# Loads of two blocks moved to the ScalarE queue, and the first store moved up behind its Silu, in an RMSNorm + SiLU kernel

One core of one Trainium2 chip. The metric is the device time of one execution in microseconds (us), the median of several; lower is better.

## The reference

```python
# x: (8, 1024, 2048) float32, gamma: (2048,) float32, eps = 1e-5
rms = np.sqrt(np.mean(x ** 2, axis=-1, keepdims=True) + eps)
out = gamma * x / rms
return out * (1 / (1 + np.exp(-out)))
```

67.11 MB are read and 67.11 MB written; every element is used once.

## The kernel before

The 8192 rows are cut into 16 blocks of 4 MB (128 partitions x 4 rows x 2048). Six buffers hold blocks; a block is loaded, worked on in place and stored. The ring of buffers ties the two ends together: block b + 6 may be loaded only when block b has been stored.

```python
def load(b):
    xt = pool.tile([P, J * d], f32, name="xt")          # 6 buffers
    nc.sync.dma_start(out=xt, in_=xb[b])                # SyncE's queue
    blocks[b] = xt

def sums(b, after_first=()):                            # sums of squares
    ...                                                 # 1 or 2 rows on VectorE, 2 or 3 on ScalarE (Square)
        if j == 0:
            for s in after_first:
                store(s)                                # behind the block's first Square
    ...                                                 # rstd = (ss / d + eps) ** -0.5 on GpSimd

def finish(b, halves=False):
    ...                                                 # VectorE: x * rstd * gamma; ScalarE: Silu, 2 rows at a time

def store(b):
    nc.scalar.dma_start(out=ob[b], in_=blocks[b])       # ScalarE's queue
    if b + LEAD < nblk:                                 # LEAD = 6
        load(b + LEAD)

# start: five loads, gamma on ScalarE's queue, then load 5
for b in range(BUFS - 1):
    load(b)
...
sums(0); finish(0); sums(1)
for b in range(1, last - 1):
    sums(b + 1, after_first=[b - 1])
    finish(b)
...                                                     # the last block is stored in two halves
```

## Time and profile before

| | |
|---|---|
| time, first three runs | 317.98 us median (317.71 to 318.61) |
| span of the profiled run | 316.6 us |
| bytes moved | 134.24 MB, mean 424 GB/s |
| busy: VectorE, ScalarE, GpSimd | 67%, 60%, 20% |
| DMA packets' time, both queues | 98.7% of 16 engines' span |

The line of DMA shows for each fortieth of the span how busy the 16 DMA engines were, in tenths; below it is what they moved. It reads 9 nearly everywhere here, so the DMA engines are what binds, although compute engines wait too. The prediction shows these lines. In the views SPq and ACTq are the sequencers of SyncE and ScalarE, which issue the DMAs; "Square" and "Silu" are ScalarE's two operations (L68 and L86).

### The profile page before, as it was taken

What the parts mean: (1) busy time and instruction counts of PE and PEld (TensorE: products, weight loads), DVE (VectorE), ACT (ScalarE), POOL (GpSimd) and SP (SyncE); (2) the same over time, 40 slices, a digit from 0 to 9 for tenths busy, and PEclk for the clock granted to TensorE, in tenths of its full rate; (3) what the DMA queues carried; (4) which work ended last, traced back from release to release, by engine and by line L of the source; (5) the groups of instructions that cost most, each with busy time, mean ns of one, the idle gap of its engine ahead of it and who ended that gap; (6) DMA issues with size and microseconds to landing.
All of it is one profiled execution on the core that took longest, in us unless ns stands there. A gap on an engine that the chain in (4) does not pass through costs nothing.

```text
span 316.6 us, 446 instructions
## 1 busy us (share of the span) xinstructions
PE 2.1 (1%) x8; PEld 0.5 (0%) x8; DVE 212.5 (67%) x122; ACT 190.2 (60%) x107; POOL 64.6 (20%) x37
## 2 busy tenths in 40 slices
PE   0200000000000000000000000000000000000000
PEld 0000000000000000000000000000000000000000
DVE  0688599996772947929485393975929369985600
ACT  1338978688774285473778436567368754782800
POOL 0010160514040601506004060330602106001000
DMA  8999999999999999999999999999999999999995
GB/s 332 414 447 431 431 397 443 418 447 414 447 414 455 411 448 414 447 439 422 435 426 439 431 435 426 451 414 447 426 435 435 426 435 426 435 431 439 426 429 242
DMA packets 4762, 134.24 MB, mean 424 GB/s; under 512 B 532, under 2 KB 532, under 8 KB 536
## 3 DMA queue, kind: packets, MB, share of 16 engines
q1 hardware_dynamic: 2304, 67.11, 49.5%
q10 hardware_dynamic: 2456, 67.12, 49.2%
q14 instruction: 2, 0.02, 0.0%
HBM read 67.12 MB, written 67.11 MB: 424 GB/s over the span
## 4 chain that ended last, share of the span: by engine, by line
DMA 59%; DVE 15%; issue 4%; ACT 3%; DVEq 1%; POOL 0%; POOLq 0%; ACTq 0%; SPq 0%
DMA xt<-in_x_dram 35%; DMA out_dram<-xt 24%; DVE xt L82 13%; ACT xt L86 2%; DVE junk_v L64 1%; ACT junk_a L68 1%; DVEq L158 1%; POOLq L158 0%; POOL rstd L77 0%; ACTq L91 0%; DVE ss L64 0%; POOL var L74 0%; ACTq L68 0%; SPq L52 0%; DVEq L82 0%
## 5 line engine op out<-in xcount | busy, mean ns | idle before, releaser
L86 ACT ACTIVATE xt<-xt 128x4096 f32<-128x4096 f32 x32 | 115.7, 3617 | 71.4 <-DVE xt L82 71.4
L82 DVE SCALAR_TENSOR_TENSOR xt<-xt,rstd,g 128x2048 f32<-128x2048 f32 x64 | 146.1, 2346 | 8.7 <-POOL rstd L77 8.7
L64 DVE CUSTOM_DVE_ANT_0 junk_v<-xt 128x2048 f32<-128x2048 f32 x28 | 64.4, 2299 | 66.4 <-DMA xt<-in_x_dram 66.0
L68 ACT ACTIVATE junk_a<-xt 128x2048 f32<-128x2048 f32 x36 | 67.7, 1880 | 39.0 <-DMA xt<-in_x_dram 37.9
L74 POOL TENSOR_SCALAR var<-ss 128x4 f32<-128x4 f32 x16 | 22.4, 1401 | 222.1 <-DVE ss L64 117.5
L77 POOL TENSOR_TENSOR rstd<-var,half 128x4 f32<-128x4 f32 x16 | 41.9, 2621 | 1.3
L112 DVE COPY g<-junk_v 128x2048 f32<-128x2048 f32 x1 | 2.3, 2292 | 9.3 <-PE junk_v L110 9.3
L68 ACT ACTIVATION_READ_ACCUMULATOR junk_a<-xt 128x1 f32 x36 | 6.7, 186 | 0.0
L64 DVE DVE_READ_ACCUMULATOR2_ANT ss<- 128x1 f32 x28 | 3.9, 141 | 0.0
L110 PE MATMUL junk_v<-xt,ones 1*128 1x512 f32 x8 | 2.1, 1133 | 8.1 <-DMA xt<-in_gamma_dram 8.1
L105 ACT ACT_TABLE_LOAD x1 | 1.3, 1283 | 0.7 <-PEq L144 0.7
L86 ACT ACT_TABLE_LOAD x1 | 1.3, 1283 | 0.0
L103 DVE MEMSET ones<- 128x128 f32 x1 | 0.2, 165 | 0.8 <-PEq L144 0.8
L110 PEld LDWEIGHTS junk_v<-xt,ones 1*128 1x128 f32 x8 | 0.5, 305 | 8.1 <-issue 8.1
L105 ACT ACTIVATE junk_a<-ones 128x1 f32<-128x1 f32 x1 | 0.2, 174 | 0.0
L104 POOL MEMSET half<- 128x4 f32 x1 | 0.1, 101 | 0.3 <-POOLq L144 0.3
L144 POOL MEMSET const-float32-0.0<- 128x1 f32 x1 | 0.1, 98 | 0.2 <-issue 0.2
L144 POOL MEMSET const-bfloat16-1.0<- 128x1 bf16 x1 | 0.1, 101 | 0.0
L144 POOL MEMSET const-uint8-127<- 128x1 uint8 x1 | 0.1, 101 | 0.0
L144 POOL MEMSET const-float32-1.0<- 128x1 f32 x1 | 0.1, 99 | 0.0
## 6 DMA issues: line engine op xcount, KB each, us to landing
xt<-in_x_dram SPq DMA_DIRECT2D x16, 4096.0 KB, 36.9
out_dram<-xt ACTq DMA_DIRECT2D x15, 4096.0 KB, 40.1
out_dram<-xt ACTq DMA_DIRECT2D x2, 2048.0 KB, 14.0
xt<-in_gamma_dram ACTq DMA_DIRECT2D x1, 8.0 KB
```

What stands on the lines that cost most here:

```text
L64: nc.vector.tensor_tensor_reduce(out=junk_v, in0=row(b, j), in1=row(b, j), scale=1.0, scalar=0.0, op0=ALU.mult, op1=ALU.add, accum_out=ss[ ...
L68: nc.scalar.activation(out=junk_a, in_=row(b, j), func=ACT.Square, accum_out=ss[:, j:j + 1])
L74: nc.gpsimd.tensor_scalar(out=var, in0=ss, scalar1=1.0 / d, scalar2=float(eps), op0=ALU.mult, op1=ALU.add)
L77: nc.gpsimd.tensor_tensor(out=rstd, in0=var, in1=half, op=ALU.pow)
L82: nc.vector.scalar_tensor_tensor(out=row(b, j), in0=row(b, j), scalar=rstds[b][:, j:j + 1], in1=g, op0=ALU.mult, op1=ALU.mult)
L86: nc.scalar.activation(out=blocks[b][:, cols], in_=blocks[b][:, cols], func=ACT.Silu)
L103: nc.vector.memset(ones, 1.0)
L105: nc.scalar.activation(out=junk_a[:, 0:1], in_=ones[:, 0:1], func=ACT.Square)
L110: nc.tensor.matmul(junk_v[:, c * w:(c + 1) * w], ones[k:k + 1, :], grow[k:k + 1, 0:w], start=True, stop=True)
L112: nc.vector.tensor_copy(out=g, in_=junk_v)
L144: nc = _bacc.Bacc("TRN2", target_bir_lowering=False, num_devices=1)
L158: with _tile.TileContext(nc) as tc:
```

## The change

The intent: keep both DMA queues at work all the time. Before, ScalarE's queue carried nothing but gamma until the first store at 38 us. Now it carries blocks 1 and 3, and the first store comes right behind them as soon as its Silu is done.

```diff
-    def load(b):
+    def load(b, queue=None):
         xt = pool.tile([P, J * d], f32, name="xt")
-        nc.sync.dma_start(out=xt, in_=xb[b])
+        (queue or nc.sync).dma_start(out=xt, in_=xb[b])
...
-        for b in range(BUFS - 1):
-            load(b)
+        load(0)
...                                    # gamma's load on ScalarE's queue
+        for b in range(1, BUFS - 1):
+            load(b, nc.scalar if b in (1, 3) else nc.sync)
...
         sums(0)
         finish(0)
+        store(0)
         sums(1)
         for b in range(1, last - 1):
-            sums(b + 1, after_first=[b - 1])
+            sums(b + 1, after_first=[b - 1] if b > 1 else [])
```

## The prediction

> **What bounds the kernel now.** I read the page from the top: busy shares, slices of DMA, share of the two queues, and the chain of waits.
>
> ```profile
> PE 2.1 (1%) x8; PEld 0.5 (0%) x8; DVE 212.5 (67%) x122; ACT 190.2 (60%) x107; POOL 64.6 (20%) x37
> ...
> DMA  8999999999999999999999999999999999999995
> GB/s 332 414 447 431 431 397 443 418 447 414 447 414 455 411 448 414 447 439 422 435 426 439 431 435 426 451 414 447 426 435 435 426 435 426 435 431 439 426 429 242
> ...
> q1 hardware_dynamic: 2304, 67.11, 49.5%
> q10 hardware_dynamic: 2456, 67.12, 49.2%
> ...
> DMA 59%; DVE 15%; issue 4%; ACT 3%; DVEq 1%; POOL 0%; POOLq 0%; ACTq 0%; SPq 0%
> ```
>
> No compute engine is near full (VectorE 67%). The DMA digit is 9 in all slices but the first and the last, and the queues' packets take 49.5 + 49.2 = 98.7% of sixteen engines' span. The queue q1 is SyncE's (loads, 67.11 MB), q10 ScalarE's (gamma and stores, 67.12 MB). So the bound is moved bytes: 134.24 MB. The waits of the two sides confirm it: compute waits for loads, and SyncE, which issues the loads, waits for stores to free the buffers.
>
> ```profile
> DVE junk_v L64 <- DMA xt<-in_x_dram: 66.0, 12, 8.0
> ACT junk_a L68 <- DMA xt<-in_x_dram: 37.9, 11, 10.9
> ...
> SPq L52 <- DMA out_dram<-xt: 225.0, 10, 52.9
> ```
>
> Next I cut the span into stretches, to see where the DMA engines lose time (columns: stretch, its us, busy us and instructions of PE, PEld, DVE, ACT, POOL, then clock, DMA share, GB/s).
>
> ```profile
> 0.00:2.00 2.00, 0.00 (x0) 0.00 (x0) 0.17 (x1) 1.28 (x1) 0.29 (x5) 1.00 0.66 180
> 2.00:6.00 4.00, 0.00 (x0) 0.00 (x0) 0.00 (x0) 0.17 (x1) 0.00 (x0) 1.00 0.75 311
> ...
> 179.00:256.00 77.00, 0.00 (x0) 0.00 (x0) 52.40 (x30) 46.83 (x26) 19.02 (x8) 1.00 1.00 432
> ...
> 312.00:317.00 5.00, 0.00 (x0) 0.00 (x0) 0.00 (x0) 0.00 (x0) 0.00 (x0) 1.00 0.24 102
> ...
> 14.00:38.00 24.00, 0.00 (x0) 0.00 (x0) 19.99 (x14) 17.36 (x13) 1.21 (x2) 1.00 1.01 436
> 38.00:46.00 8.00, 0.00 (x0) 0.00 (x0) 6.44 (x3) 5.95 (x7) 4.76 (x4) 1.00 0.99 389
> 46.00:102.00 56.00, 0.00 (x0) 0.00 (x0) 42.42 (x25) 42.10 (x23) 14.06 (x7) 1.00 1.00 432
> ```
>
> The steady rate is about 433 GB/s, and it is the same with one queue working (436 in 14 to 38 us, loads alone) as with two (432). At 433 GB/s the bytes need 134.24 / 0.433 = 310.0 us. The span is 316.6, so 6.6 us are lost, and the stretches say where. **Start**: 0 to 6 us moved 2 x 180 + 4 x 311 = 1604 KB, worth 3.7 us, so 2.3 lost. **End**: 312 to 316.6 moved 510 KB, worth 1.2 us, so 3.4 lost. **A dip**: 38 to 46 us at 389 GB/s loses 8 x (433 - 389) / 433 = 0.8 us. Sum 6.5. The dip stands exactly where the first store is issued, onto a ScalarE queue that had carried only gamma:
>
> ```profile
> 33.90 0.18 ACT L68 ACTIVATION_READ_ACCUMULATOR junk_a<-xt 128x1 f32 x1
> ...
> 38.23 1.88 ACT L68 ACTIVATE junk_a<-xt 128x2048 f32<-128x2048 f32 x1
> ...
> 38.28 0.36 ACTq L91 DMA_DIRECT2D out_dram<-xt  x1
> ```
>
> That is the one loss in mid-run, and it bears on what the change is for.
>
> **What the Trainium skill says.** "DMA: Bandwidth & Descriptors", section "Issuing engines are not separate DMA queues": DMAs of all issuing engines end on the same 16 DMA engines and interleave; several issuers save only issue time. The trace agrees: 436 GB/s with one queue, 432 with two. The same page, "Queues, rings and completion order": each DMA engine takes turns between the queue rows it has work for, packet by packet. The trace agrees in that the steady stage gives a load of 4 MB a median of 36.9 us from issue to landing while the first load, alone, took 12.3. The same page, "Bandwidth", gives a fabric ceiling of 435 GB/s; the measured 433 leaves almost nothing between. No page that I found tells what the first transfer on an idle queue costs; the dip is only the trace's.
>
> **The change part by part.**
>
> 1. Blocks 1 and 3 go to ScalarE's queue, behind gamma; SyncE keeps 0, 2, 4 and 5. This adds two issues on ScalarE at about 0.34 us each (the stores' issue there is 338 ns), in the first 3 us when ScalarE waits for data until 13.09 anyway: nothing on the path. The bytes and their rate stay. But the order of arrival changes. A block alone takes 4.194 MB / 0.433 = 9.7 us; two queues taking turns bring two blocks in 19.4. Block 0, which landed at 13.1 alone, had perhaps 1 to 2 us alone ahead of block 1's start, so I expect it at 21 to 22 us, and block 1 some 1 us later; blocks 2 and 3 at 41 to 42. So the first sums start 8 us later.
>
> 2. The first store. Before, block 0's last Silu started at 28.58 and took 3.62, done at 32.2, 19.1 us after landing; its store waited until 38.28 behind four Squares of blocks 1 and 2, the first of which waited for ScalarE's turn at 32.10. Now it stands right behind the Silu: 21.4 + 19.1 = about 40.5 us. So it comes 2 us later, not earlier, in spite of being moved up. It costs nothing in DMA: loads fill the engines until about 60 us (six blocks of 9.7, plus the start). Block 3's tail on the ScalarE queue runs to about 42, and the store's packets, perhaps 2 us after issue (the estimate is from the first load, issued at 0.72 and moving within 2 us), would be there at about 42.4. So the queue is handed over nearly without a gap; I can't tell which side of zero.
>
> 3. The following stores. In the new order ScalarE does three Squares of block 1 (3 x 2.05 us), then two of block 2, Silu of block 1 and a Square of block 3 before store 1: rstd of block 1 at about 48.4, four VectorE passes to 57.5, second Silu done at about 61.2, store 1 issued at about 61.4 (52.38 before). Store 0 moves from 42.4 to 42.4 + 19.4 = 61.8, so store 1's packets may come 1 to 2 us after the ScalarE queue ran dry. Load 5 alone then keeps the engines busy; no bytes are lost except by a second dip, if waking a queue is what costs. By the same counting store 2 is issued at about 75 against a need at 82, store 3 at 89 against 102: compute has caught up.
>
> 4. From about 100 us on both kernels run the same loop. Store 0 lands at about 62 in both, so load 6 goes out at the same time, and the order of instructions on all engines is the same from the second store on.
>
> 5. The tail: the last two half stores were issued at 296.93 and 301.45, while the earlier stores had work until about 303, so the engines stayed full to 312. I expect the same slack of some 7 us.
>
> Sum: bytes 0; issue 0; later first compute 0, hidden under loads; dip between -0.8 (gone) and +0.8 (a second one); start -0.3 to +0.5 (two queues ramp together, or the second disturbs the first). My centre is half the dip won: 317.98 - 0.4 = **317.6 us**.
>
> **The rivals.**
>
> *A: the dip is the price of waking the ScalarE queue, and it vanishes into the start.* For it: the packets' rate falls exactly after the issue at 38.28, no later store makes such a stretch, and rates are lowest at the start too, where the other queue wakes. Then -0.8 us: 317.2.
>
> *B: the dip is the price of the first write, or of a mixture of reads and writes beginning, or it comes with the wake wherever that is.* Against it speaks only that I see no reason in the trace. Then it moves to 42 us or to 3 us, and the time is the same: 318.0.
>
> *C: the delayed compute of block 0 hits the path: the ScalarE queue runs dry, SyncE has no free buffer, both queues idle.* For it: 8 us of delay in the first landing, and store 1 nine us later. Against it: two blocks of loads (19 us) are still queued when store 0 starts, one remains when it ends. If I am wrong by some 10 us there, it would cost a few us: 320 to 323.
>
> *D: two queues really move more than one.* It would need more than the 432 of the mixed stage; the loads alone show 436. Worth at most 1% of 40 us, 0.4 us.
>
> **Range and chances.** The three times of before span 317.71 to 318.61, so noise alone is about half a microsecond. Between A with some of D (316.8) and B with a second dip (318.8) lies nearly everything; C has perhaps one chance in twenty. Faster by over 2% needs 6.4 us, and all that is lost besides bytes is 6.6, most of it start and end that the change leaves: 1%. Slower by 2% needs C in a bad form: 2%. Within 2%: 97%.
>
> **What would show it right or wrong.** Step 1: the first Square at 21 to 22 us instead of 13.09. Step 2: the first store's issue at 40 to 41. Step 3: the second at 60 to 62. Step 4: SyncE's waits for stores as large as before, and the DMA digit 9 throughout. The dip: GB/s in 38 to 46 us; 430 or more says A, about 390 says B; a new dip near 62 to 68 says that a queue that ran dry pays again. Step 5: the last store issued at about 301. The prediction is wrong if a digit under 9 shows up between 20 and 300 us (C), or if the mean rate in mid-run differs from 432.

## The result, and the profile after

After: 318.52 us median (318.36 to 319.36, 6 runs); before, over the six runs to that point: 318.38 us (317.71 to 319.63). The ratio is 1.0006, 95% interval 0.9985 to 1.0028: the same. Here and below a ratio is the mean time of one kernel's fast runs over that of the other's of the same rounds, so it is not quite the ratio of the medians.

The page of the changed kernel, to be held against the same lines of before:

```profile
DMA  8999999999999999999999999999999999999996
...
q10 hardware_dynamic: 2744, 75.51, 55.3%
q1 hardware_dynamic: 2016, 58.72, 43.6%
```

The two loads did move: 8.4 MB went from q1 (SyncE) to q10 (ScalarE). The sum of the shares is 98.9% against 98.7% before. There was no idle share to win.

The order of events in the changed kernel, from the timeline (start, duration, engine, line, operation):

```profile
20.25 1.88 ACT L68 ACTIVATE junk_a<-xt 128x2048 f32<-128x2048 f32 x1 [18.07 <-DMA xt<-in_x_dram]
...
35.74 3.62 ACT L86 ACTIVATE xt<-xt 128x4096 f32<-128x4096 f32 x1 [0.91 <-DVE xt L82]
...
39.38 0.36 ACTq L91 DMA_DIRECT2D out_dram<-xt  x1
...
60.09 0.35 ACTq L91 DMA_DIRECT2D out_dram<-xt  x1
```

Block 0 shares the engines with block 1 and lands at 20.25 instead of 13.09 us. Its store, although moved up in the program, is issued at 39.38, later than the 38.28 of before; the second store at 60.09 instead of 52.38. None of this costs anything, because the loads that are still queued keep the engines full (the six loads alone last until about 60 us; here, beside store 0, until 76).

The stretches that the prediction used (last column GB/s):

```profile
14.00:38.00 24.00, 0.00 (x0) 0.00 (x0) 16.12 (x10) 11.16 (x7) 1.21 (x2) 1.00 1.01 437
38.00:46.00 8.00, 0.00 (x0) 0.00 (x0) 4.72 (x4) 7.42 (x8) 0.05 (x1) 1.00 0.99 393
...
179.00:256.00 77.00, 0.00 (x0) 0.00 (x0) 51.28 (x31) 45.79 (x25) 19.01 (x8) 1.00 1.00 432
```

Two queues of loads move 437 GB/s where one moved 436. The dip near the first store is still there.

**A finer ruler for the dip.** A packet of a block is one row of 32 KB, and an 8 us stretch holds only some 100 of them, so its GB/s depends on how many happen to start inside. The queue lines of a stretch give something better. They tell packets, MB and the packets' time as a share of 16 engines times the stretch. For 8 us that is 128 engine-us: share x 128 / (MB / 0.032768) is the mean time of one packet. Packets under 512 bytes, which take almost no time, are left out of the count. First a quiet stretch of before, 70 to 78 us, then its dip, 38 to 46 us (16 of q1's 81 packets are under 512 bytes):

```profile
q10 hardware_dynamic: 51, 1.67, 48.4%
q1 hardware_dynamic: 50, 1.64, 47.4%
```

```profile
q1 hardware_dynamic: 81, 2.13, 70.3%
q10 hardware_dynamic: 30, 0.98, 28.4%
```

Quiet: 0.474 x 128 / 50 = 1.21 us a packet on q1, the same on q10. Dip: q1's 65 large packets took 90.0 us, 1.38 each. The store's own packets (q10) took 1.21. So the loads in flight are slowed while the first store comes in, by 90.0 - 65 x 1.213 = 11.1 engine-us, or **0.70 us** as a mean over the 16 engines. The changed kernel, 42 to 50 us (16 small ones on q10):

```profile
q1 hardware_dynamic: 57, 1.87, 64.6%
q10 hardware_dynamic: 55, 1.28, 37.1%
```

By the same working, 0.84 us. The dip went with the first store and did not shrink, although ScalarE's queue now has work ahead of the store. I call this number the *extra* below. It is not peculiar to stores: in all fourteen kernels the very first packets of the loads bear one of 0.5 to 0.8 us (before, 1 to 4 us: 30 packets, 95.9%, which gives 0.60 us).

### The profile page after: what moved, and what is told of

Read it like the earlier page. It is cut to its first block, busy times and chain, and to the rows that moved or that the text cites. A ratio compares the mean times of both kernels' runs of the same rounds, so it can differ in the third digit from the quotient of the medians.

```text
span 316.6 us, 445 instructions
## 1 busy us (share of the span) xinstructions
PE 2.1 (1%) x8; PEld 0.5 (0%) x8; DVE 212.4 (67%) x122; ACT 189.9 (60%) x107; POOL 62.8 (20%) x37
## 4 chain that ended last, share of the span: by engine, by line
DMA 49%; DVE 18%; ACT 6%; issue 6%; DVEq 1%; POOL 0%; POOLq 0%; another core or an unknown queue 0%; ACTq 0%; SPq 0%
DMA out_dram<-xt 29%; DMA xt<-in_x_dram 20%; DVE xt L82 15%; ACT xt L86 4%; ACT junk_a L68 2%; DVE junk_v L64 2%; DVEq L162 1%; POOLq L162 0%; POOL rstd L77 0%; DVE ss L64 0%; POOL var L74 0%; ACTq L91 0%; DVEq L82 0%; SPq L52 0%
## 5 line engine op out<-in xcount | busy, mean ns | idle before, releaser
L77 POOL TENSOR_TENSOR rstd<-var,half 128x4 f32<-128x4 f32 x16 | 40.0, 2497 | 1.3
```

The costliest lines, as they stand in the source:

```text
L77: nc.gpsimd.tensor_tensor(out=rstd, in0=var, in1=half, op=ALU.pow)
```

## The experiments

Twelve kernels ran; "before" is timed in the same rounds.

**1 and 2: each half of the change alone.** The first is the diff without `store(0)` and its condition, the second is only these:

```diff
         finish(0)
+        store(0)
         sums(1)
-            sums(b + 1, after_first=[b - 1])
+            sums(b + 1, after_first=[b - 1] if b > 1 else [])
```

> Only the first half of the change: blocks 1 and 3 loaded on the ScalarE queue, the stores where they were. My theory (bytes bind; the DMA engines are full with one queue as with two): same time as before within 0.5%, the dip of about 0.8 us still there in the stretch where the first store's packets begin (about 40 to 60 us), first Square at about 20 us, first store issued some us later than 39.4 because it stands behind the Squares of block 1. Rival (two queues move more than one): 14 to 38 us above 436 GB/s and over 0.5 us won.

> Only the second half: the first store right behind its Silu, all loads on SyncE. First store issued at about 32.2 instead of 38.28. My theory: same time within 0.5%; the dip moves with the store, to 32 to 40 us, and keeps its size of 0.8 us. Rival (an earlier first store gives back its 6 us, or the dip is tied to the loads): over 1 us faster, or the dip stays at 38 to 46 us.

Measured: loads alone 317.73 us, ratio 0.9992 (0.9975 to 1.0008); store alone 318.0 us, ratio 1.0000 (0.9983 to 1.0017); before 317.87. The first store was issued at 45.34 and at 32.27 us, and the extra lay at 44 to 52 us (0.77) and at 32 to 40 us (0.57). The lines of the second, 32 to 40 us:

```profile
q1 hardware_dynamic: 64, 2.10, 67.8%
q10 hardware_dynamic: 32, 1.05, 30.3%
```

So the halves don't cancel each other: neither gains or loses anything beyond the 0.2% or so that the intervals allow, over 13 us of difference in when the first store goes out. The dip moved with the store, as expected.

**3: the first three stores held back.**

```diff
-            sums(b + 1, after_first=[b - 1])
+            sums(b + 1, after_first={1: [], 2: [], 3: [0, 1, 2]}.get(b, [b - 1]))
```

> The reverse of the change: stores 0, 1 and 2 all issued behind the first Square of block 4, at about 66 us. Loads last until about 61 us, so from there to about 68 us neither queue has work. My theory: that hole and nothing else counts: 6 to 7 us slower (324 to 325), less the dip, which may be hidden in the hole. Rival (an idle ScalarE queue costs by itself): 28 us of idling more would cost more than the hole, or the hole would not be the place.

Measured: 321.8 us, ratio 1.0121 (1.0106 to 1.0136): slower by 3.9 us, not by 6 to 7. The size was off because stores 0 and 1 were issued at 62.53, not 66 us, although in the program they stand behind block 4's first Square, which started at 65.91: ScalarE's sequencer did not wait for it. The hole in the stretches of this run:

```profile
60.00:62.00 2.00, 0.00 (x0) 0.00 (x0) 2.00 (x2) 1.48 (x1) 0.96 (x1) 1.00 0.00 0
62.00:64.00 2.00, 0.00 (x0) 0.00 (x0) 2.00 (x2) 1.61 (x1) 0.00 (x0) 1.00 0.62 262
```

Against 433 GB/s the two lines lost 2.0 + 0.8 us. That is the place where most of the time is lost: where *both* queues are dry. Up to 60 us the idling of ScalarE's queue, 22 us longer than before, cost nothing: 433 GB/s from 14 to 60 us. A second thing appeared. The first store, coming in with no load beside it, shows next to no extra (62 to 70 us: 1.23 us a packet), but when loads come back among the stores, at 74 to 82 us, the extra is 1.2 us, some 0.5 more than before pays. With the 2.8 us of the hole that is most of the 3.9 us:

```profile
q10 hardware_dynamic: 64, 2.10, 71.9%
q1 hardware_dynamic: 30, 0.98, 31.8%
```

Here q10's packets, those already running, took 0.719 x 128 / 64 = 1.44 us.

**4 and 9: everything on one queue.** Loads and stores on SyncE's queue, in run 4 all but the last two halves, in run 9 those too.

```diff
-        nc.scalar.dma_start(out=ob[b], in_=blocks[b])
-        if b + LEAD < nblk:
-            load(b + LEAD)
+        nc.sync.dma_start(out=ob[b], in_=blocks[b])
+        if b >= 1 and b - 1 + LEAD < nblk:
+            load(b - 1 + LEAD)             # one store further on, so that SyncE never waits with an empty queue
```

> All loads and all stores but the last two halves go through SyncE's queue, so ScalarE's queue is idle for some 295 of 316 us. My theory: two queues or one make no difference as long as one always has work: within 0.5% of before, about 432 GB/s in the middle, the dip still there at the first store. Rival (both queues must be kept busy): several per cent slower, with a lower rate in the middle.

> As the earlier run with one queue, but the last two half stores go through SyncE's queue too, so that ScalarE's queue carries gamma only. That run was 1% slower, and its loss lay in the end: the two halves shared the engines with the stores still queued on the other queue, and the last DMA engine ended some 5 us behind most. Theory (two queues are not needed; the end's sharing made the 1%): within 0.4% of before. Rival (one queue is slower by itself): 1% slower again, now with the loss in the middle.

Measured: 321.05 us, ratio 1.0095 (1.0078 to 1.0113), and 321.69 us, ratio 1.0113 (1.0090 to 1.0135). My theory missed both times: one queue is 1% slower by itself, and my reading of run 4, that the shared end made the loss, fell with run 9. The rate of the middle is nearly what it was, so it is not the later issue of the loads either: 432 and 429 GB/s in two stretches of 77 us. The loss shows at the end. Share of the DMA engines (the column before the last) in the last microseconds, first before, then run 9:

```profile
313.00:314.00 1.00, 0.00 (x0) 0.00 (x0) 0.00 (x0) 0.00 (x0) 0.00 (x0) 1.00 0.16 66
314.00:315.00 1.00, 0.00 (x0) 0.00 (x0) 0.00 (x0) 0.00 (x0) 0.00 (x0) 1.00 0.08 33
315.00:316.00 1.00, 0.00 (x0) 0.00 (x0) 0.00 (x0) 0.00 (x0) 0.00 (x0) 1.00 0.00 0
```

```profile
313.00:314.00 1.00, 0.00 (x0) 0.00 (x0) 0.00 (x0) 0.00 (x0) 0.00 (x0) 1.00 0.35 148
314.00:315.00 1.00, 0.00 (x0) 0.00 (x0) 0.00 (x0) 0.00 (x0) 0.00 (x0) 1.00 0.27 115
315.00:316.00 1.00, 0.00 (x0) 0.00 (x0) 0.00 (x0) 0.00 (x0) 0.00 (x0) 1.00 0.19 82
316.00:317.00 1.00, 0.00 (x0) 0.00 (x0) 0.00 (x0) 0.00 (x0) 0.00 (x0) 1.00 0.15 66
```

0.35 of 16 is between five and six engines. Each transfer of a block ends with 16 packets of 4 bytes (one for each engine, as I read it), so these tell when the engines finish. At 314 to 319 us, first before, then run 9:

```profile
DMA packets 5, 0.04 MB, mean 8 GB/s; under 512 B 2, under 2 KB 2, under 8 KB 2
DMA packets 21, 0.28 MB, mean 56 GB/s; under 512 B 4, under 2 KB 4, under 8 KB 4
```

In run 9 twelve engines end by 313.6 us, as in before, and four at 316.2 to 318.1; in before the last ends at 315.3. The last engine sets the time. The single packets of the kept trace (`prof` shows their sums) tell where they fell behind. From 70 to 290 us run 9's large packets have 15.5 engine-us above 1.213 us each, before's 4.3, and nearly all of it lies in some forty packets, most of which come every 19 or 20 us, where a store follows a load in the queue. The sixteen small packets of one transfer lie 0.4 us apart at 41 us, 2.9 at 168 and 5.0 at 265; the median engine stays within 0.4 us of the first. Run 4 shows the same. So with one queue, as I read it, a few engines pay again at each change from load to store, and that adds up. Why only a few do was not tested.

**5 to 8: does a small transfer ahead pay for the dip?** The kernel before plus one transfer of 64 KB (128 rows of 512 bytes) behind gamma, in four kinds:

```diff
+        nc.scalar.dma_start(out=scratch, in_=ones)                      # run 5: SBUF to a scratch tensor in HBM
+        nc.scalar.dma_start(out=ob[nblk - 1][:, 0:P], in_=ones)         # run 6: SBUF to the output
+        nc.scalar.dma_start(out=scratch, in_=xb[0][:, 0:P])             # run 7: HBM to HBM
+        nc.scalar.dma_start(out=ones2, in_=ones)                        # run 8: SBUF to SBUF
```

> The kernel before plus one store of 64 KB (128 rows of 512 bytes, SBUF to a scratch tensor in HBM) on ScalarE's queue right behind gamma. Theory W (the dip is the price of the engines' first write to HBM): the dip at 38 to 46 us goes, 430 GB/s or more there, and the time falls by up to 0.8 us or the loss moves into 0 to 14 us. Theory S (first read of SBUF by a DMA): the same here. Theory O (the first touch of the output's memory): dip stays at about 390. Theory L (a large transfer in the other direction beginning): stays.

> The same small store, into the output itself (128 columns of the last block, overwritten at the end). W and S: the dip goes. O: the dip goes here and only here if the price is paid once per tensor; if it is paid per piece of memory it stays. L: stays.

> A copy of the same size from x in HBM to a scratch tensor in HBM: a write to HBM without a read of SBUF. W: the dip goes. S: it stays. O and L: it stays.

> A copy of the same size from SBUF to SBUF: a read of SBUF without a write to HBM. S: the dip goes. W, O and L: it stays at about 390 GB/s in 38 to 46 us.

Measured: 317.81, 318.23, 318.08 and 317.7 us, before 318.07; ratios 0.9973 to 0.9987, all intervals holding 1. The extra at 38 to 46 us stayed in all four: 0.67, 0.63, 0.78 and 0.59 us. So W, S and O, as I put them, are out: none of these small transfers pays the price in advance. O's other form, a price per piece of memory, does not fit either: later stores write fresh memory too, and the large packets of before, from 70 to 290 us, have an extra of only 0.27 us in all. L is the one left.

**10: a load, not a store, opens the idle queue.** Load 5 goes out on ScalarE's queue; in the program it stands behind block 0's second Silu. SyncE's queue is busy then.

```diff
-        load(BUFS - 1)                     # on SyncE's queue
         finish(0)
+        load(BUFS - 1, nc.scalar)
         sums(1)
```

> The kernel before, with block 5 loaded by ScalarE's queue at about 32 us, when that queue has been idle for 25 us and SyncE's is busy. The first store then finds the ScalarE queue busy and starts at about 55 us. Theory R (opening an idle queue beside a busy one costs the 0.7 us, whatever the direction): a dip in 33 to 39 us, when the load begins, and none at the first store. Theory D (the first store among loads costs it): no dip at 33 to 39 us, one where the first store begins. If R and D both hold, both dips. The time within 0.5% of before in any case.

Measured: 319.05 us, ratio 1.0035 (1.0020 to 1.0050). The load was issued at 28.63 us. Queue lines at 32 to 40 us, when its packets flow beside the other loads, and at 48 to 56 us, when the first store comes in:

```profile
q1 hardware_dynamic: 51, 1.64, 47.4%
q10 hardware_dynamic: 50, 1.64, 47.4%
```

```profile
q1 hardware_dynamic: 64, 1.57, 52.2%
q10 hardware_dynamic: 64, 1.57, 47.8%
```

The first pair is 1.21 us a packet on both queues: no extra. (In the second, the 32 packets under 512 bytes must be left out; 1.57 MB are 48 large ones, and they took 1.39 and 1.28 us, an extra of 0.73.) So R fell: opening an idle queue beside a busy one was free where both carried loads; the changed kernel had shown the same, ScalarE's queue being opened by load 1 at 2 us. SyncE's queue ran dry later in this run, and when loads came back among stores, at 70 to 86 us, there was a second extra of 0.31 + 0.39 = 0.70 us; the stretch cuts it short, and at 70 to 90 us it is 1.0 us. That is as in run 3, and it fits the 1.1 us (0.35%) that this kernel is slower.

**11 and 12: a large store ahead.** 16 rows of 32 KB from block 0, as soon as it has landed: on the idle ScalarE queue in the kernel before (11), between loads 1 and 3 in the changed kernel (12).

```diff
+        nc.scalar.dma_start(out=scratch, in_=blocks[0][0:16, :])
```

> The kernel before plus one store of 16 rows of 32 KB (512 KB, one packet of the stores' size for each DMA engine) of block 0 to a scratch tensor, issued at 13 us on the idle ScalarE queue. The bytes alone are worth 1.2 us. Theory F (the price is paid once, by the first store of full-size packets): a dip at 14 to 20 us, none at 38 to 46 us, total loss as before. R and D (paid at each opening of an idle queue, or at each change from loads alone to loads and stores): dips at both, some 0.7 us more on top of the 1.2.

> The changed kernel with the same 512 KB store on ScalarE's queue between loads 1 and 3, issued at 20 us when block 0 has landed, so that the queue doesn't run idle. F: a dip at about 20 to 27 us, none at 42 to 50 us where the first real store begins. D: a dip at both. R: a dip at neither. Time: 1.2 us for the bytes, and 0, 0.7 more or 0.7 less.

Measured: 333.46 us (331.69 to 336.47), ratio 1.0498 (1.0439 to 1.0557), and 320.75 us (319.82 to 321.59), ratio 1.0088 (1.0062 to 1.0114). On the question asked, the answer agrees in both. The queue lines where the first block's store comes in, at 46 to 54 us in run 11 and at 42 to 50 us in run 12:

```profile
q10 hardware_dynamic: 56, 1.84, 53.1%
q1 hardware_dynamic: 49, 1.61, 46.4%
```

```profile
q1 hardware_dynamic: 56, 1.84, 55.2%
q10 hardware_dynamic: 55, 1.61, 46.5%
```

In run 11 the packets took 1.21 us: no extra. In run 12 the extra is 0.16 us, against the changed kernel's 0.84. The small store itself had 1.4 and 1.6 us of it. So F is the theory that these two runs bear out, and D as I had put it (at each change from loads alone to both) fell. Two limits: here the extra lay mostly on the small store's own packets, 2.5 and 2.7 us each, and not on the loads beside it, so it may be another cost; and runs 3, 9 and 10 show the price paid more than once. It is not a way to win either, as the early store cost more than it saved.

And run 11 missed its expected time by far: 15.6 us slower, where the bytes are worth 1.2. The early store landed only 10.5 us after its issue, and since block 0 is worked on in place, VectorE waited 5.7 us for it. After it the whole run was a little slower (425 GB/s at 102 to 179 us, 431 in the changed kernel), and the end lost the overlap. This is the end of run 11:

```profile
304.00:312.00 8.00, 0.00 (x0) 0.00 (x0) 8.00 (x4) 3.62 (x1) 0.00 (x0) 1.00 0.66 283
```

At 304 to 312 us a third of the engines' time is empty, though stores remain: block 14 had been landed at 270.5 instead of 256.2 us, so the last block's compute ended late (its half stores were issued at 311.19 and 315.71, in before at 296.93 and 301.45). Why block 14 came so late can be read from its sixteen small packets: they lie at 253.6 to 270.1 us, in before at 254.8 to 255.8. The first engine was not late; the last was, and a block has landed only when the last has finished. This spread was 0.8 us at load 0, 2.5 at load 1, just after the early store, 5.8 at load 4, and grew to 16.5; all large packets of run 11 together have 6.6 us above 1.213 each (mean over the engines), before's 1.6. What in one odd store of 16 partitions starts this drift, and why it grows in run 11 and hardly in run 12 (3.0 to 4.8 us), is open.

## Why the prediction was right

The time, 318.5 us, lies in the range, and "same" was right. The number tests little more than that: the range is 2 us wide, and before itself moved from 317.98 to 318.38 between its first three runs and all six. Between A (317.2), the centre (317.6) and B (318.0) only the traces decide.

- **The bound.** Right. Bytes over a rate that one queue already reaches: 436 GB/s with one, 437 with two. Run 3 shows what a stretch with both queues dry costs (2.8 us). One limit: "the same with one queue as with two" holds for the rate but not for the whole run, since runs 4 and 9 are 1% slower through a few late engines. And the 36.9 us that the prediction gives a load as a sign of taking turns includes the wait behind the load ahead on the same queue; the 51 and 50 packets of the two queues at 70 to 78 us are the better sign.
- **Step 1**, first Square at 21 to 22 us: measured 20.25. I gave block 0 too short a time alone ahead of block 1: load 1's packets began 4.4 us after load 0's, not 1 to 2. So block 1 landed at 26.9 us, some 7 us after block 0 and not 1.
- **Step 2**, the store issued at 40 to 41: 39.38, for that same reason; later than before, as said. The hand-over without a gap came true, but by a later tail: block 3's ran to 47, not to 42. And a first store's packets begin later than my 2 us after the issue: in before 4.7 us after it (38.28 to 43.02).
- **Step 3**, second store at 60 to 62: 60.09. The second dip that I feared did not come.
- **Step 4**, the same loop from 100 us on: SyncE's waits for stores add up to 228.0 us, before to 225.0, and 102 to 179 us move 431 GB/s, before 432. Store 0 did not land at the same time, though: load 6 was issued at 67.2 us, before at 63.5. It cost nothing, as the engines had other work.
- **Step 5**, the last store at about 301: 300.11, in before 301.45; the engines stayed full until 312.
- **The sum.** My centre of 317.6 gave half the dip as won. None was: the extra is 0.84 us against 0.70. Rival A fell (the changed kernel and run 10), B was right in that the price moved and stayed. The measured difference of the medians is 0.1 us.
- **Rivals C and D.** No slice between 20 and 300 us shows a digit under 9, so C is out, and 437 against 436 leaves D nothing.

Where the expected gain went: it was never there. A queue is a place to wait, and the 16 engines behind it were busy with the other queue's loads. The dip that could have justified the change comes where full-size stores first meet loads, and it moves with the first store. What makes that price is open: in runs 11 and 12 an early store of full-size packets takes it away or most of it. Being out of step can hardly be the whole reason in run 12: the sixteen small packets of the load just ahead of the first store lie 3.6 us apart there and 3.6 us in the changed kernel, which pays 0.84 all the same. Nor is it told why loads that return among stores pay it again (runs 3 and 10), and why in one queue all engines pay at the first store (0.77 us at 56 to 64 us in run 9) and later only a few.

## What to carry to other kernels

Ask of a DMA-bound kernel whether the *engines* idle, not whether a queue does: moving loads to the second queue, or a first store by 13 us, gained nothing here while the other queue had work. Look at the last microseconds engine by engine, because a few engines that end late cost about 3 us here, and a queue that stood idle 22 us longer beside a busy one cost nothing. And measure a suspected dip by the time of one packet, since the GB/s of a short stretch depends on where it is cut.

## What the Trainium skill lacked or had wrong

- "DMA: Bandwidth & Descriptors", "Issuing engines are not separate DMA queues", says that issuing from several engines only saves the sequencer's time to initiate. Its main statement agrees with the runs (436 and 437 GB/s). But all on one queue was 1.0 to 1.1% slower at nearly equal rates in the middle, through four DMA engines that ended at 316.2 to 318.1 us, the rest by 313.6 (run 9); I found nothing there on engines that drift apart when loads and stores share a queue.
- No page that I found has the price of the first full-size store among loads: 0.57 to 0.84 us, mean over the engines, in the kernels without an early large store in which that store met running loads. Four kinds of 64 KB transfers ahead did not take it away.
- "DMA: Bandwidth & Descriptors", "Rules for kernel authors", advises 128 partitions and at least 1 MiB for a DMA. The 4 MB blocks over 128 partitions did move 432 GB/s; size and partitions were not varied apart. The page doesn't say what a transfer that breaks the advice can cost those that follow: one 512 KB store from 16 partitions took 10.5 us to land and made the kernel 15.6 us slower in one place, and with its surroundings changed (run 12) about 2.9 us. After the first of them the engines' ends of one transfer drifted from 2.5 to 16.5 us apart.
